# A planner's order for a hybrid decoder layer: corrected prices, and 260 listed shifts of its priorities

## The chip, the core and the metric

The kernel runs on one core of a Trainium2 chip. A core has five engines that matter here, each with its own row of instructions that it runs strictly in order: PE (TensorE, matmuls; its weight loads are shown apart as PEld), DVE (VectorE), ACT (ScalarE), POOL (GpSimd) and SP (SyncE, which here does nothing but issue DMA transfers). Engines wait for one another by semaphores. The metric is the device time of one execution in microseconds (us), the median over several runs.

## The reference, cut to what matters

One decoder layer over a prompt of 2048 tokens and 64 sample tokens (8 sequences of 8, which continue caches of 2048 keys). One input projection feeds two mixers; their gated outputs are joined by one output projection.

```python
h = rmsnorm(x, norm_w)
z = h @ w_in
q, k, v, qb, kb, vb, g_lr, gate_a, gate_b = jnp.split(z, split_points(), axis=-1)
q = rope(rmsnorm(heads(q, H_A), q_norm_w), pos)          # 8 heads x 64
k = rope(rmsnorm(heads(k, H_A), k_norm_w), pos)
o_a = attend(q, k, v)       # windows (128, 1), (512, 4), (2048, 16), joined by their softmax denominators
log_a = jax.nn.log_sigmoid(g_lr @ w_gate_up + b_gate) / GATE_TAU
o_b, s_fin = gla_chunked(qb * DK_B ** -0.5, kb, vb, log_a, s0)   # gated linear attention, 4 heads
o_b = rmsnorm(o_b, gla_norm_w)
mixed = jnp.concatenate([o_a * silu(gate_a), o_b * silu(gate_b)], axis=-1)
y = x + mixed @ w_out
```

Beside y the layer returns the new keys and values and the GLA states.

## The kernel before

**Tiles.** The prompt is cut into 16 tiles of 128 tokens, and "s" is the tile of the sample. Activations and weights are split into two fp16 parts, high and low, so each projection takes three products per 128 rows of depth: high x high, high x low, low x high (L1745). The projections come in the blocks q, k, v, qkb (queries and keys of the GLA), g (gate a and the low-rank gate), vb and gb (gate b); their sums are acc_q, acc_k and so on. Weights are loaded as f32 (wr_...), scaled, and written by ACT (L1275) and DVE (L1276) as w_....

**Attention.** Rotated q and k go to memory (qp_d, kp_d) and come back transposed by SP: kk (L1457) and qq (L1471) for branches 1 and 2, in four slabs m = 0 to 3 of 512 tokens; T_q and T_k (L1556, L1558) for the 16 residues of branch 3. A unit is s (scores, PE, L1025), mask and exponential (DVE L1033, ACT L1036), t (transposes on PE, L1043), a split into fp16 parts (ACT, DVE or POOL), O (PE, L1058), and a store to o_d.

**Dots.** The sample's scores over its cached keys are no matmuls. For each sequence and step SP loads a row of queries to all partitions (qb, L1610) and blocks of keys (k, L1612 and L1615); POOL multiplies (pr, L1600) and DVE adds up (sck, L1601). There are 128 such dots.

**GLA.** Eight pieces e0 to e7 of 256 tokens, and one of the sample. The decays are seven steps of POOL (kq_e, L839) with PE's scores between (sc_e, L872). Each 128-token chunk ends in O_0 to O_15 (PE, L1911 and L1917), a norm over ACT and DVE (gla_out, L909 to L916: osq, oss, rr, ob_c), and a store to ob_d (L917).

**Output.** For each tile, combine(t) (L2122 to L2165) loads the three branch results (oc, L2125), the GLA result (obl), and the two gates (gwl, gal), weighs them on DVE, ACT and POOL, and writes mix; parts_of splits it (mt, L2063 and L2064), PE transposes it (tm, L2073), and Y (L2108) is the output projection. The sample's attention over its cached values (R L2291, OS L2357, values sv_b) is woven in between.

**What sets the order.** All instructions are recorded first. Then the class Plan reads their dependences, gives each a price (busy: how long its engine is held; late: when its result is there; lands: for a DMA, the time from the end of its bytes to its signal), and makes a list schedule. order runs a model of the five engines and picks, whenever one is free, the ready instruction with the smallest priority. backward runs the same from the end and gives new priorities, the latest place of each instruction. settle repeats the two and returns an order for each engine; fix then ties each engine's instructions into that order. Nothing of the computation is touched. In the kernel before, settle makes eight rounds, plays each order on four copies of the program with randomly lengthened prices (other, replay), and keeps the best:

```python
    plan = Plan(tc, nc)
    plan.fix(plan.settle(8, 500.0, 1.2, 50.0, 10.0))
```

## Time and profile before

| | |
|---|---|
| runs | 1297.75, 1304.37, 1305.67 us; median 1304.37 |
| profiled execution | 1306.69 us, of which 1304.9 us span from its first to its last instruction |
| mean granted PE clock | 0.986 |
| PE busy | 1222.5 us, 94% |
| DVE, ACT, POOL busy | 961.1 us (74%), 819.1 us (63%), 551.1 us (42%) |
| HBM | 198 GB/s over the span |

The profile is of one execution. A line number is that of the kernel before; in the kernel after, the lines behind the planner's prices stand 3 further down (L1457 is L1460, L2108 is L2111). A busy PE is one with a matmul in its pipeline, which is not always PE at its peak. A wait is put down to the engine or transfer that came last. The order of the span is: projections q, k, v to about 160 us, attention with the qkb and g projections as filler to about 815, GLA with vb and gb as filler to about 1040, output projection with the sample's attention to the end.

### The profile page before, as it was taken

Reading aid. Unit: us, or ns where it says so; the run is one execution under the profiler, and the core shown is the slowest. Engines: PE = TensorE matmul, PEld = TensorE weight load, DVE = VectorE, ACT = ScalarE, POOL = GpSimd, SP = SyncE. Lnnn points to the kernel's source line nnn. Section 1 sums busy time; section 2 is a strip of 40 time slices with the busy share of each in tenths; the row PEclk is TensorE's granted clock in tenths of the full one; section 3 lists DMA queues with packets and bytes.
Section 4 is the critical chain, followed back from the end, with each engine's and each line's share of the span. In section 5 each row is a group of like instructions: output and inputs, shape, how many; then the busy total and the mean of one; then the engine's idle time right before and its main releaser. Section 6 shows DMA issues by size and latency. Waiting matters only on the chain.

```text
span 1304.9 us, 26224 instructions
## 1 busy us (share of the span) xinstructions
PE 1222.5 (94%) x8942; PEld 726.2 (56%) x8942; DVE 961.1 (74%) x2450; ACT 819.1 (63%) x2191; POOL 551.1 (42%) x475
## 2 busy tenths in 40 slices
PE   4999989999998989999999999999999959999998
PEld 2444465666576556766666656665665425445443
DVE  7897888989889648777778558787778485567641
ACT  6655598888499759968678435678788532223220
POOL 0145435555655225643434777545433142233410
PEclk9999999999999989999999999999999969999999
DMA  8579945876944977799999877554335499989822
GB/s 293 187 212 247 252 152 114 223 190 196 218 133 143 222 226 252 228 253 274 260 245 245 246 206 202 156 171 149 118 118 171 146 330 397 342 331 364 297 94 75
DMA packets 235833, 283.09 MB, mean 217 GB/s; under 512 B 116193, under 2 KB 146866, under 8 KB 232626
## 3 DMA queue, kind: packets, MB, share of 16 engines
q1 hardware_dynamic: 235698, 281.40, 72.2%
q8 instruction: 71, 1.16, 0.4%
q14 instruction: 64, 0.52, 0.1%
HBM read 183.02 MB, written 75.24 MB: 198 GB/s over the span
## 4 chain that ended last, share of the span: by engine, by line
PE 36%; DVE 9%; DMA 8%; ACT 7%; issue 4%; POOL 4%; SPq 1%; DVEq 0%; POOLq 0%; ACTq 0%
PE Y L2108 11%; PE acc_qkb L1745 5%; PE acc_gb L1745 3%; POOL pr L1600 2%; PE OS L2357 2%; PE acc_vb L1745 2%; ACT p L1036 2%; PE s L1025 2%; PE t L1043 1%; PE acc_g L1745 1%; PE O L1058 1%; DMA oc<-o_d 1%; DMA qb<-q_d 1%; DMA T_q<-qp_d 1%; PE sc_e L872 1%
## 5 line engine op out<-in xcount | busy, mean ns | idle before, releaser
L1600 POOL TENSOR_TENSOR pr<-k,qb 128x512 f32<-128x512 f32 x128 | 166.8, 1303 | 190.8 <-DVE sck L1601 107.9
L1745 PEld LDWEIGHTS <-hr 128*128 128x128 f16 x1824 | 174.2, 99 | 115.1 <-issue 12.2
L1036 ACT ACTIVATE p<-p,o 128x256 f32<-128x256 f32 (+1 forms) x384 | 172.7, 454 | 39.9 <-DVE o L1033 35.7
L1745 PEld LDWEIGHTS <-hl 128*128 128x128 f16 x1248 | 119.5, 98 | 120.9 <-issue 9.2
L2108 PE MATMUL Y<-w_o,mh 128*128 128x512 f16 x768 | 181.4, 381 | 1.9 <-ACT mh L2074 1.4
L1010 POOL TENSOR_TENSOR pt<-p,pt 128x512 f16<-128x512 f32 (+1 forms) x80 | 95.1, 1190 | 109.8 <-ACT pt L1009 91.1
L1058 PE MATMUL O<-v,pt 128*128 128x128 f16 x1200 | 131.0, 219 | 10.0 <-POOL pt L1010 3.5
L1043 PE MATMUL t<-ident,p 128*128 128x128 f32 x600 | 125.3, 283 | 2.4 <-ACT p L1036 1.0
L1601 DVE TENSOR_REDUCE sck<-pr 128x8 f32<-128x512 f32 x128 | 87.1, 680 | 54.9 <-POOL pr L1600 54.5
L2108 PEld LDWEIGHTS <-mh 128*128 128x128 f16 x768 | 71.9, 98 | 85.4 <-issue 9.8
L1745 PE MATMUL acc_g<-w_g,hr 128*128 128x256 f16 (+1 forms) x768 | 117.4, 277 | 0.5 <-DVE za L1447 0.2
L1745 PE MATMUL acc_v<-w_v,hl 128*128 128x512 f16 x384 | 115.7, 384 | 2.3 <-ACT zs_q L1320 1.5
L1058 PEld LDWEIGHTS <-pt 128*128 128x128 f16 x1200 | 92.0, 98 | 42.8 <-POOL pt L1010 8.1
L1745 PE MATMUL acc_k<-w_k,hl 128*128 128x512 f16 x384 | 110.4, 379 | 0.5 <-DVE vp L1407 0.5
L1745 PE MATMUL acc_q<-w_q,hl 128*128 128x512 f16 x384 | 107.1, 379 | 2.1 <-DVE za L1447 1.1
L1745 PE MATMUL acc_vb<-w_vb,hr 128*128 128x512 f16 x384 | 103.5, 382 | 4.8 <-DVE so_g L1294 4.8
L1033 DVE CUSTOM_DVE_ANT_0 p<-s,m3w,scl_s 128x128 f32<-128x128 f32 (+1 forms) x256 | 88.4, 394 | 15.8 <-PE s L1025 7.1
L1745 PE MATMUL acc_gb<-w_gb,hr 128*128 128x512 f16 x384 | 96.0, 383 | 0.0
L2156 POOL TENSOR_TENSOR tc<-oc,w 128x512 f32<-128x512 f32 x32 | 44.2, 1400 | 112.7 <-DVE w L2148 67.4
L1025 PE MATMUL s<-kk,qq 128*128 128x256 f16 (+1 forms) x512 | 82.8, 268 | 8.7 <-DMA kk<-kp_d 4.7
L1043 PEld LDWEIGHTS t<-ident,p 128*128 128x128 f32 x600 | 74.8, 141 | 28.4 <-ACT p L1036 12.4
L1745 PE MATMUL acc_qkb<-w_qkb,hr 128*128 128x512 f16 x288 | 79.0, 383 | 0.1
(528 smaller groups left out, 2545.7 us busy)
## 6 DMA issues: line engine op xcount, KB each, us to landing
k<-in_cache_k_win SPq DMA_DIRECT2D x104, 256.0 KB
sv_b<-in_cache_v_win SPq DMA_DIRECT2D x24, 1024.0 KB
hr<-h_d SPq DMA_DIRECT2D x44, 512.0 KB
qb<-q_d SPq DMA_DIRECT2D x64, 256.0 KB
oc<-o_d SPq DMA_DIRECT2D x48, 264.0 KB
o_d<-o SPq DMA_DIRECT2D x64, 132.0 KB
x<-in_x_prompt SPq DMA_DIRECT2D x16, 512.0 KB
h_d<-hl SPq DMA_DIRECT2D x16, 512.0 KB
```

What stands on the lines that cost most here:

```text
L1010: POOL.tensor_tensor(l, f, h, ALU.subtract)
L1025: PE.matmul(s_ps[:, i * w : (i + 1) * w], q, k, start=(n == 0), stop=(n == len(prods) - 1),)
L1033: DVE.tensor_tensor_reduce(s[:, sl], s_ps[:, sl], mask, neg, BIG, ALU.add, ALU.min, nmf(i))
L1036: ACT.activation(s[:, sl], s[:, sl], AF.Exp, bias=nmf(i), scale=-1.0, accum_out=denf(i))
L1043: PE.transpose(p_ps[:, i * P : (i + 1) * P], t["s"][:, i * P : (i + 1) * P], ident[:])
L1058: PE.matmul(o_, t["pt"][:, c, (i * nb + b) * P : (i * nb + b + 1) * P], vf(i, b), start=(n == 0), stop=(n == 2 * nb - 1),)
L1600: POOL.tensor_tensor(pr[:], kt, qt, ALU.mult)
L1601: DVE.tensor_reduce(out, pr[:].rearrange("p (u k d) -> p u k d", u=2, k=4), AX.X, ALU.add)
L1745: PE.matmul(z, a_[:, k, :], w[:, p_, k, cols], start=(k == 0 and i == 0), stop=(k == KT - 1 and i == 2),)
L2108: PE.matmul(Y[:], a_[:, k, :], w_[:, part, k, :512], start=(i == 0), stop=(i == len(prods) - 1),)
L2156: eng.tensor_tensor(t_[:], oc[:, g, :, 0:64], w[:, g].unsqueeze(2).to_broadcast([P, NH, HD]), ALU.mult,)
L2357: PE.matmul(OS[32 * x : 32 * x + 32, 0:256], ps(x), vs_[bb][:, 256 * u : 256 * u + 256], start=(i == 0), stop=(i == 13),)
```

## The change

Prices in Plan.price are corrected: the bytes of a transposing DMA and its landing are shorter; a DMA with one row spread to all partitions costs 3.16 times as much; the others depend on whether they write to memory and how long their rows are; a DVE instruction with two 16-bit inputs is 110 ns later; DVE and ACT are held 5 ns longer; and POOL's cheap case is told by the innermost dimension alone.

The perturbed copies (other, replay) and the choice among rounds go. settle now makes seven rounds with slightly other margins, and then goes through a list of 260 numbers. Each number seeds a generator that draws one instruction and one of four sets: all instructions that belong to the same tile (half of the draws), the instruction alone, the instructions of its engine within a reach of 10 to 100 us that write tiles of the same kind, or all of its engine within that reach. The priorities of the set are shifted together by a normal number times 1, 3, 10 or 30 us. After all shifts one order is made and fixed. The program is the same instruction for instruction; only the five rows are other.

```diff
--- before.py
+++ after.py
@@ -320,8 +320,8 @@
                 if kind == "InstDmaTransposeAnt":
                     total = cells(ts[0]) * ts[0].ap[0][1] * 2
                     busy = 1400.0 if total < 500000 else 2800.0
-                    late = 18.0 * total / 256 / 16
-                    self.lands[len(self.busy)] = 2200.0
+                    late = 11.2 * total / 256 / 16
+                    self.lands[len(self.busy)] = 1900.0
                 else:
                     nd = max(
                         len([x for x in list(a.ap) if x[1] != 1]) for a in (ts[0], os_[0])
@@ -331,7 +331,14 @@
                     total = cells(os_[0]) * list(os_[0].ap)[0][1]
                     total *= 2 if os_[0].dtype in (F16, BF16) else 4
                     late = total / r / 16 * (7 + r * 0.0377)
-                    self.lands[len(self.busy)] = 2300.0 if space(os_[0]) == "DRAM" else 2900.0
+                    if space(os_[0]) == "DRAM":
+                        more, lands = 0.98, 1870.0
+                    elif list(ts[0].ap)[0][0] == 0:
+                        more, lands = 3.16, 1700.0
+                    else:
+                        more, lands = (1.05, 2390.0) if r >= 4096 else (1.11, 2325.0)
+                    late *= more
+                    self.lands[len(self.busy)] = lands
                 busy += 25
                 late *= self.traffic
             else:
@@ -364,12 +371,14 @@
                     else:
                         late = (205 if by_row else 145) + (0.52 if sbuf else 1.042) * n
                         lock = sbuf
-                    busy = late - 80
+                    if len(wide) >= 2 and all(a.dtype in (F16, BF16) for a in wide):
+                        late += 110
+                    busy = late - 75
                 elif e == "Activation":
                     late = (160 if space(ts[0]) == "PSUM" else 190) + 0.836 * cells(o) if ts else 60
                     if len([a for a in ts[1:] if cells(a) == 1]) and cells(o) > 1:
                         late += 90
-                    busy = late - 105
+                    busy = late - 100
                     if len(os_) > 1:
                         busy += 92
                         late += 85
@@ -381,7 +390,10 @@
                     elif kind == "InstTensorCopy":
                         late = 130 + 1.0 * n
                     else:
-                        spread = any(s == 0 and c > 1 for a in ts for s, c in list(a.ap)[1:])
+                        spread = any(
+                            d[-1][0] == 0
+                            for d in ([x for x in list(a.ap)[1:] if x[1] > 1] for a in ts) if d
+                        )
                         half = any(a.dtype in (F16, BF16) for a in ts)
                         late = 180 + (1.68 if spread else 1.92 if half else 2.12) * n
                     busy = late - 45
@@ -622,55 +634,46 @@
                 released(x)
         return place
 
-    def other(self, seed):
+    def moved(self, seed):
 
         import random
 
-        r, q = random.Random(seed), Plan.__new__(Plan)
-        q.__dict__.update(self.__dict__)
-        q.late, q.busy, q.lands = list(self.late), list(self.busy), dict(self.lands)
-        for n in range(self.real):
-            if self.eng[n] == "SP":
-                q.late[n] *= 0.4 + 0.6 * r.expovariate(1)
-                q.lands[n] += 400 * (r.expovariate(1) - 0.5)
-            elif self.eng[n] != "PE":
-                more = r.choice((0, 0, 0, 30))
-                q.late[n] += more
-                q.busy[n] += more
-        return q
-
-    def replay(self, out):
-
-        q = Plan.__new__(Plan)
-        q.__dict__.update(self.__dict__)
-        q.then, q.behind = [list(x) for x in self.then], [set(x) for x in self.behind]
-        for order in out.values():
-            for a, b in zip(order, order[1:]):
-                if a not in q.behind[b]:
-                    q.behind[b].add(a)
-                    q.then[a].append(b)
-        return q.order([0.0] * len(self.dep), 0.0)[0]
-
-    def settle(self, rounds, land, traffic, cross, bias, others=4):
-
-        true = Plan.__new__(Plan)
-        true.__dict__.update(self.__dict__)
+        r = random.Random(seed)
+        n, kind = r.randrange(self.real), r.random()
+        by = r.gauss(0, 1) * r.choice((1e3, 3e3, 1e4, 3e4))
+        if kind < 0.5:
+            return self.mates[self.leaf[n]], by
+        if kind < 0.6:
+            return [n], by
+        reach, own = r.choice((1e4, 3e4, 1e5)), self.stem[n]
+        return [
+            x for x in range(self.real)
+            if self.eng[x] == self.eng[n] and abs(self.base[x] - self.base[n]) < reach
+            and (kind > 0.85 or self.stem[x] == own)
+        ], by
+
+    def settle(self, rounds, land, traffic, cross, bias, steps):
+
         self.rank()
-        true.nxt, true.then = self.nxt, self.then
-        others = [true.other(k) for k in range(others)]
         self.lands = {n: x + land for n, x in self.lands.items()}
         self.late = [
             x * (traffic if self.eng[n] == "SP" else 1.0) for n, x in enumerate(self.late)
         ]
         self.cross = cross
-        prio, best = [-f for f in self.rank()], None
+        prio = [-f for f in self.rank()]
         for _ in range(rounds):
-            out = self.order(prio, bias)[1]
+            self.order(prio, bias)
             prio = [-x for x in self.backward(self.start)]
-            end = sum(o.replay(out) for o in others)
-            if best is None or end < best[0]:
-                best = end, out
-        return best[1]
+        self.leaf = [next((t for t, w, m in reversed(a) if w), "?") for a in self.acc]
+        self.stem = [t.rstrip("_0123456789") for t in self.leaf]
+        self.mates, self.base = {}, list(prio)
+        for n, t in enumerate(self.leaf):
+            self.mates.setdefault(t, []).append(n)
+        for seed in steps:
+            some, by = self.moved(seed)
+            for x in some:
+                prio[x] += by
+        return self.order(prio, bias)[1]
 
     def fix(self, out):
 
@@ -2417,8 +2420,43 @@
 
         weave(out, [sample_attention(), 4 * 9])
 
+    steps = (
+        798993397, 379503271, 976436735, 990016090, 697217584, 129675417, 778155539, 369111627,
...
+        933499419, 856040043, 620662419, 525063118, 526738383,
+    )
     plan = Plan(tc, nc)
-    plan.fix(plan.settle(8, 500.0, 1.2, 50.0, 10.0))
+    plan.fix(plan.settle(7, 600.0, 1.15, 60.0, 10.0, steps))
 
 
 # ---- launch: one core; inputs and outputs as the reference has them ----
```

**Place 1: the end of the gb projection.** On PE, the last matmuls of the last GLA chunk, O_15 (O_13304), among the gb matmuls. acc_gb_13985 is gb tile 12, acc_gb_14061 gb tile 13; tiles 14 and 15 follow. Before:

```order
L1745 LDWEIGHTS hr_13839
L1745 MATMUL acc_gb_14061<-w_gb,hr_13839 128x512
L1917 MATMUL O_13304<-vb_13297,full 128x128 x2
L1745 LDWEIGHTS hr_13839
L1745 MATMUL acc_gb_14061<-w_gb,hr_13839 128x512
L1745 LDWEIGHTS hr_13839
L1745 MATMUL acc_gb_14061<-w_gb,hr_13839 128x512
```

After:

```order
L1748 LDWEIGHTS hr_13798
L1748 MATMUL acc_gb_13985<-w_gb,hr_13798 128x512
L1914 MATMUL O_13304<-Sbd_9605,kq_e_13053 128x256
L1920 MATMUL O_13304<-vb_13297,full 128x128 x2
L1914 MATMUL O_13304<-Sbd_9605,kq_e_13053 128x256
L1920 MATMUL O_13304<-vb_13297,full 128x128 x2
L1748 LDWEIGHTS hr_13798
L1748 MATMUL acc_gb_13985<-w_gb,hr_13798 128x512
```

O_15 stands one gb tile earlier. Up to the first output transpose 52 gb matmuls follow it before, 90 after.

On SP, the same place: ob_c_13329 is the result of O_15, oc_13929 with obl, gwl and gal the loads of the first combine, gw_14097 the finished gate of gb tile 13, gw_14022 of tile 12. Before:

```order
L1391 DMA gw_d<-gw_14022 128x512
L917 DMA ob_d<-ob_c_13329 128x512
L1391 DMA gw_d<-gw_14097 128x512
L2125 DMA oc_13929<-o_d 128x528 x3
L2128 DMA obl_13934<-ob_d 128x512
L2130 DMA gwl_13936<-gw_d 128x512
L2132 DMA gal_13938<-ga_d 128x512
L2125 DMA oc_14025<-o_d 128x528 x2
```

After:

```order
L1394 DMA gw_d<-gw_13918 128x512
L920 DMA ob_d<-ob_c_13329 128x512
L2276 DMA Sc_15377<-sc_d 128x2x128
L2128 DMA oc_13929<-o_d 128x528 x3
L2131 DMA obl_13934<-ob_d 128x512
L1394 DMA gw_d<-gw_14022 128x512
L2133 DMA gwl_13936<-gw_d 128x512
L2135 DMA gal_13938<-ga_d 128x512
```

The loads oc and obl stand right behind the store of O_15 and one load for the sample (Sc); the store of gate 13 is no longer ahead of them.

**Place 2: the keys of the last slab, m = 3.** On SP, T_q and T_k for branch 3, qq and kk for branches 1 and 2. Before:

```order
L1556 DMA_TRANSPOSE T_q_7921<-qp_d 128x8x128
L1558 DMA_TRANSPOSE T_k_7923<-kp_d 128x8x128
L1457 DMA_TRANSPOSE kk<-kp_d 128x8x128
L1517 DMA o_d<-o_2_1_2_6115 128x264
L1517 DMA o_d<-o_2_1_3_6204 128x264
L1502 DMA v_3_0_2_6867<-vp_d 128x512
L1373 DMA zqk_d<-zq_6592 128x512
L1182 DMA hr_6776<-h_d 128x2048
L1471 DMA_TRANSPOSE qq_1_7049<-qp_d 128x4x128
L1562 DMA v_0_7814<-vp_d 128x1024
L1457 DMA_TRANSPOSE kk<-kp_d 128x8x128
```

After:

```order
L1559 DMA_TRANSPOSE T_q_7797<-qp_d 128x8x128
L1460 DMA_TRANSPOSE kk<-kp_d 128x8x128
L1185 DMA hr_6440<-h_d 128x2048
L1376 DMA zqk_d<-zq_6249 128x512
L1505 DMA v_3_0_0_6670<-vp_d 128x512
L1561 DMA_TRANSPOSE T_k_7799<-kp_d 128x8x128
L1474 DMA_TRANSPOSE qq_1_7049<-qp_d 128x4x128
L1460 DMA_TRANSPOSE kk<-kp_d 128x8x128
L1520 DMA o_d<-o_2_1_1_5940 128x264
L1561 DMA_TRANSPOSE T_k_7923<-kp_d 128x8x128
```

Before, the last two kk stand behind both T_k's. After, the third stands ahead of both, and the last (row 385 of SP before, 375 after) between them.

**Place 3: the first decay of the GLA.** On POOL, kq_e_10021 is piece e0 in decay, pr are the dots (pr_7_4 is sequence 7, step 4), and Ac_e, prod_e and gT_e belong to the GLA too. Before:

```order
L1600 TENSOR_TENSOR pr_7_0_7903<-k_7_0_7899,qb_0_7897 128x512
L1600 TENSOR_TENSOR pr_7_0_7906<-k_7_0_7901,qb_0_7897 128x512
L839 TENSOR_TENSOR kq_e_10021<-kq_e_10021,d_e_10050 128x256
L1600 TENSOR_TENSOR pr_7_4_8007<-k_7_4_8005,qb_4_8003 128x512
L839 TENSOR_TENSOR kq_e_10021<-kq_e_10021,sums_e_10053 128x128x2
L1600 TENSOR_TENSOR pr_7_4_8010<-k_7_0_7901,qb_4_8003 128x512
L839 TENSOR_TENSOR kq_e_10021<-kq_e_10021,sums_e_10053 128x64x4
L791 MEMSET gT_e_11313 17x256
L773 TENSOR_TENSOR prod_e_10875<-zqk_e_10871 128x512
L839 TENSOR_TENSOR kq_e_10021<-kq_e_10021,sums_e_10053 128x32x8
L1600 TENSOR_TENSOR pr_7_1_8110<-k_7_1_8106,qb_1_8104 128x512
L839 TENSOR_TENSOR kq_e_10021<-kq_e_10021,sums_e_10053 128x16x16
```

After:

```order
L842 TENSOR_TENSOR kq_e_10021<-kq_e_10021,d_e_10050 128x256
L783 TENSOR_TENSOR Ac_e_10448<-ident_9596,dd_e_10446 128x512
L1603 TENSOR_TENSOR pr_6_6_7629<-k_6_6_7627,qb_6_7625 128x512
L1603 TENSOR_TENSOR pr_6_6_7632<-k_6_2_7529,qb_6_7625 128x512
L842 TENSOR_TENSOR kq_e_10021<-kq_e_10021,sums_e_10053 128x128x2
L1603 TENSOR_TENSOR pr_6_3_7721<-k_6_3_7717,qb_3_7715 128x512
L794 MEMSET gT_e_11313 17x256
L776 TENSOR_TENSOR prod_e_10875<-zqk_e_10871 128x512
L842 TENSOR_TENSOR kq_e_10021<-kq_e_10021,sums_e_10053 128x64x4
L1603 TENSOR_TENSOR pr_6_3_7724<-k_6_3_7719,qb_3_7715 128x512
L842 TENSOR_TENSOR kq_e_10021<-kq_e_10021,sums_e_10053 128x32x8
L1603 TENSOR_TENSOR pr_6_7_7807<-k_6_7_7805,qb_7_7803 128x512
```

The first decay stands nine rows earlier (296, not 305), and with it go earlier dots: the last three steps of sequence 6 and all of sequence 7, two dots each, now stand behind it: 22 dots, where 14 did.

31 rows, old and new, of the table steps are left out of this document.

## The prediction

> **What bounds the kernel now.** I read the busy line of the page first, then the table of stretches, the waits where TensorE is not busy, and the chain through the largest of these.
>
> ```profile
> PE 1222.5 (94%) x8942; PEld 726.2 (56%) x8942; DVE 961.1 (74%) x2450; ACT 819.1 (63%) x2191; POOL 551.1 (42%) x475
> ```
>
> PE is the bound, with 1222.5 of 1304.9 us: the other 82.4 us is all that better waits can give. The change leaves every matmul in place, so a gain has to come out of these, or out of the pipeline breaks inside the busy time. The columns below are stretch and length; busy time of PE, PEld, DVE, ACT, POOL; then the granted clock, the DMA share and GB/s.
>
> ```profile
> 130.50:163.10 32.60, 32.52 (x163) 15.36 (x161) 26.38 (x47) 18.35 (x43) 14.38 (x9) 1.00 0.95 252
> 163.10:195.70 32.60, 28.45 (x247) 19.63 (x245) 27.08 (x101) 31.28 (x114) 12.65 (x12) 1.00 0.50 152
> 195.70:228.40 32.70, 30.92 (x232) 18.70 (x230) 26.34 (x69) 26.57 (x84) 16.53 (x13) 1.00 0.53 114
> 456.70:489.30 32.60, 27.90 (x180) 17.77 (x179) 14.79 (x47) 18.64 (x55) 8.03 (x7) 0.90 0.80 226
> 815.60:1011.30 195.70, 187.95 (x1601) 117.44 (x1599) 154.02 (x391) 152.87 (x380) 84.45 (x92) 0.98 0.47 147
> 1043.90:1076.50 32.60, 16.57 (x109) 8.86 (x110) 29.34 (x60) 11.26 (x18) 15.04 (x10) 0.69 0.92 330
> 1059.00:1240.00 181.00, 178.94 (x1351) 87.14 (x1350) 118.30 (x258) 48.42 (x75) 59.71 (x44) 0.99 0.93 349
> ```
>
> The hole is at 1043.9: 16.0 us idle in one stretch, with the clock at 0.69. Next come 4.7 us at 456.7, 4.15 and 1.8 us at 163.1 and 195.7, where ACT is full (31.28 of 32.60), and 7.75 us spread over the GLA. Behind 1059 PE is full. The waits that name the two sharp holes, over 1040 to 1062 and over 465 to 472 (total, times, longest):
>
> ```profile
> PE tm L2073 <- ACT mt L2063: 17.7, 1, 17.7
> ```
>
> ```profile
> PE s L1025 <- DMA kk<-kp_d: 4.7, 1, 4.7
> ```
>
> **A. From the gb projection to the output projection.** The chain through the hole, with start, length and what ran, and SP's issues in it:
>
> ```profile
> 1029.06 9.50 PE acc_gb L1745 x44
> ...
> 1038.61 5.02 DMA oc<-o_d
> ...
> 1056.72 0.69 DVE mix L2163
> ...
> 1057.44 1.06 ACT mt L2063
> ```
>
> ```profile
> 1034.37 0.33 SPq L917 DMA_DIRECT2D ob_d<-ob_c  x1
> 1035.31 0.32 SPq L1391 DMA_DIRECT2D gw_d<-gw  x1
> 1035.68 1.39 SPq L2125 DMA_DIRECT2D oc<-o_d  x3
> ```
>
> The last GLA chunk, O_15, ends on PE at 1029.06. Its norm and store take until 1034.37, a gw store whose POOL product is late holds SP, and the loads of the first combine start at 1035.68. The first output transposes (tm) run 17.7 us after PE's last work, at 1058.8, that is 29.8 us after O_15. Nothing but gb matmuls covers this: in the old order 52 stand behind O_15, at 9.50/44 = 0.216 us each 11.2 us. The new order has 90, so 19.4 us: +8.2. In the new order SP's loads follow ob_d with one short load between, not that gw store: of the 1.31 us from ob_d to oc I take 0.6 off. And the two ACT steps of O_15's norm (rr) no longer stand behind steps of a gate each:
>
> ```profile
> 1036.45 0.72 ACT L1298 ACTIVATE sa_gb<-sa_gb,ones 128x512 f32<-128x512 f32 x1
> ```
>
> Two of these, up to 0.72 us each, make 1.2. The hole becomes 17.7 - 8.2 - 1.8 = 7.7, **A = -10**.
>
> This has a floor of its own. On DVE the last gate (so_gb15) now stands ahead of mix of tile 0, and on ACT its last step stands ahead of mt:
>
> ```profile
> 1040.29 0.75 DVE L1294 TENSOR_SCALAR so_gb<-acc_gb,wi_gb 128x512 f32<-128x512 f32 x1 [1.30 <-PE acc_gb L1745]
> ...
> 1043.15 0.69 DVE L1302 CUSTOM_DVE_ANT_0 so_gb<-so_gb,sa_gb 128x512 f32<-128x512 f32 x1
> ```
>
> From the last gb result to the end of that gate are 1043.84 - 1040.29 = 3.55 us; mix (0.69) and mt (1.06) make 5.3 us that no order of PE hides. So A lies between -12.4 and 0 (0 if the oc loads land as late after the last gb as before).
>
> The cold clock stays: 0.69 in the stretch, and a hole of 5 to 8 us I price like one of 17.7, at no change. The Trainium skill (TensorE: Matmul & The Clock Gate, "What's actually happening") says that an idle window of about 3.4 us is enough to halve the clock, and about as much work to release it; the 0.69 agrees. By that page a hole of 7.7 us saves nothing of the cold stretch, as I have it.
>
> **B. Attention, third slab of keys (m = 3).** SP's issues there, and then, from the chain, the landing of the fourth kk:
>
> ```profile
> 440.50 1.30 SPq L1457 DMA_TRANSPOSE kk<-kp_d  x1
> ...
> 447.00 3.59 SPq L1558 DMA_TRANSPOSE T_k<-kp_d  x1
> 450.64 1.31 SPq L1457 DMA_TRANSPOSE kk<-kp_d  x1
> ...
> 456.76 3.12 SPq L1558 DMA_TRANSPOSE T_k<-kp_d  x1
> 459.92 1.31 SPq L1457 DMA_TRANSPOSE kk<-kp_d  x1
> ```
>
> ```profile
> 465.79 5.30 DMA kk<-kp_d
> 471.13 1.87 PE s L1025 x8
> ```
>
> The four kk are issued at 440.5, 450.6, 459.9 and 465.8; the last lands 5.30 us later, and s starts at 471.13. The new order puts three of them ahead of both T_k's (3.59 and 3.12 us) and the fourth between them, ten rows of SP earlier than it was, since the last kp half leaves DVE earlier. But s too stands some 16 us of PE's rows earlier, with qkb matmuls moved behind it. The 4.7 us can go entirely, or come back whole as the same landing against an earlier reader. I take two thirds: **B = -3** (0 to -4.7).
>
> **C. First attention units (m = 0).** Before 163.1 ACT is busy 18.35 of 32.60, after it 31.28. The new order begins the units some 11 us of PE's rows earlier and puts the last q and k tiles and the sample's projections (matmuls without such waits) between them. The two holes sum to 5.9 us. A third of them goes: **C = -2**; at best -5, at worst +2, since the fourth kk of m = 0 is issued just before its reader and a landing of 5.30 us behind 2 to 3 us of other work costs that.
>
> **D. GLA and the dots.** POOL's dots over 815 to 915 (count, busy time, mean ns, idle before them):
>
> ```profile
> L1600 POOL TENSOR_TENSOR pr<-k,qb 128x512 f32<-128x512 f32 x11 | 14.5, 1317 | 12.0 <-DVE sck L1601 7.1 <-DMA k<-in_cache_k_win 2.7 <-DMA ga_d<-so_g 2.2
> ```
>
> Behind the first GLA decay (kq_e) 22 dots stand now instead of 14. Eight more at 1.32 us are 10.5 us in POOL's row, of which POOL is busy 84.45 of 195.70 there. They fit, and the first decay comes nine rows earlier. GLA matmuls also stand in somewhat longer runs. Of the 7.75 us idle I take a fifth: **D = -1.5** (-8 to +10.5).
>
> **E. Output stage.** Sample attention (OS) interrupts the output matmuls:
>
> ```profile
> 1107.84 0.55 PE OS L2357 x2
> ...
> 1108.93 1.86 PE OS L2357 x30
> ```
>
> Between the runs of 2 and of 30 lie 28 matmuls in 1.31 us, 0.047 us each, so a run costs about 0.46 us beside its work. OS has 26 runs on PE before and 15 after, R 7 and 12. Eleven fewer and five more are six runs, 2.8 us; shorter tm runs give no sure price. **E = -3** (-5 if only the OS runs count, +2 if only R's).
>
> The start (identity loaded first, transposes reordered) and the tail (last Y and stores, the same) I take at 0, +-1.
>
> **Sum.** -10 - 3 - 2 - 1.5 - 3 = -19.5. The profiled execution took 1306.69 (span 1304.9 and 1.8 around it): 1306.7 - 19.5 = **1287**. It lies 2.3 above the median of the runs shown, 1304.37, and a run of 1297.75 lies below both, so the median may come out at 1285; I stay with 1287. Within 1% of 1304.37 is 1291.3 to 1317.4, about what a measurement of this kernel can tell from no change.
>
> **Rivals.**
>
> *Absorbed.* The new PE order spends each gain on an earlier reader: s waits for the same landing, only sooner, the first units wait for the fourth kk, the oc loads start earlier but land in a fuller queue (DMA share 0.92). Then A is half, -5; B, D, E 0; C +2: 1306.7 - 3 = 1304, and with A kept whole 1299; I take 1301. For it: the holes at 163 and 466 are waits for data, which a shift of the order does not shorten. Against: SP's rows do move with them. Chance 0.25.
>
> *The output stage is bound by DMA.* From 1059 to 1240 it moved 349 GB/s at a share of 0.93. If only 0.07 is free, the 181 us cannot shrink below 168, which A and E do not ask; but if the sample values (sv_b) already set the pace, E is 0 and a part of A, its 6 us of earlier start, is waited for later: 1306.7 - 4 - 6.5 = 1296. Chance 0.06. The Trainium skill (DMA: Bandwidth & Descriptors, "Where 436 GB/s comes from") states about 358 GB/s per core as the limit between memory and SBUF; by it 349 leaves 3%, and 181 us could not go below 176. The trace speaks against that:
>
> ```profile
> 1076.50:1109.20 32.70, 32.45 (x333) 16.44 (x335) 18.07 (x53) 8.38 (x18) 8.39 (x7) 1.00 1.01 397
> ```
>
> That stretch moved 397 GB/s, with PE busy 32.45 of 32.70 us.
>
> *Slower: dots in front of the decays.* POOL runs in order. Over the whole execution its dots waited 36.3 us in 9 waits for their keys:
>
> ```profile
> POOL pr L1600 <- DMA k<-in_cache_k_win: 36.3, 9, 20.8
> ```
>
> If each of the eight later dots meets such a wait (4.0 us) besides its 1.3 us, the decays behind it, and the whole GLA chain to O_15, come up to 8 x 5.3 = 42 us later, at least 10.5. PE then waits within the GLA, since the gb matmuls stand behind O_15. The forecast plus 10.5 is 1298, plus 42 is 1329; it is slower from 30 us on, that is, if most of the eight wait. Three quarters of the full price gives 1319. For it: the dots' loads share SP with the GLA's. Against: only 2.7 us of such waits in 815 to 915. Chance 0.08.
>
> *More.* A at its floor (-12.4), B -4.7, C -5, D -5, E -5: 1306.7 - 32 = 1275. Chance 0.07.
>
> **How the numbers follow.** My forecast, 1279 to 1291.3, has 0.54. With "more" that is 0.61 faster; absorbed and DMA make 0.31 within 1%; 0.08 slower. The range runs from 1271, a little under "more", to 1305, the upper end of "absorbed": that leaves out the slower case and the edges. The forecast's own range is 1279 to 1296.
>
> **What would show it.** A: PE's wait for mt of tile 0 at 6 to 9 us, not 17.7, and the last gb matmuls some 19 us long behind O_15. B: the wait of s for kk at 465 gone or under 2 us. C: PE busy over 130 to 228 up by 2 us or more. D: POOL's wait for keys within the GLA still a few us, PE idle there under 8. E: fewer OS runs, the stage from first tm to the end 3 us shorter. I am wrong if the hole before tm stays above 13 us, if s waits for kk in new places by more than 3 us, or if the GLA's end lies later than before.

## The result, and the profile after

The changed kernel takes 1263.6 us (median of 4 runs, 1262.71 to 1264.7) against 1304.43 us before: a ratio of 0.970, with a 95% interval of 0.966 to 0.973. That is 41 us or 3.0% faster, where 17 us were forecast, and below the range (1271 to 1305). The two profiled executions, on which everything below rests, lie 44 us apart (spans 1304.9 and 1260.9). The kernel before, timed again beside the experiments, gave medians of 1300.6 to 1304.3 us, so a difference of 3 us between two kernels below means little; e2, e3 and e6 had one run each of 2 to 3.4 ms, which the ratios leave out.

The busy line of the page after:

```profile
PE 1202.4 (95%) x8942; PEld 723.7 (57%) x8942; DVE 956.1 (76%) x2450; ACT 817.8 (65%) x2191; POOL 549.0 (44%) x475
```

The instructions and their busy times are the same to within 1% on DVE, ACT and POOL. PE's busy time fell by 20 us, and the time in which PE is not busy by 24 (82.4 to 58.5). So only about half of the gain lies in time that the page shows as idle. The stretches of after that answer to those shown of before, with the same columns (those at 446, 791.2 and 1016.9 begin within 2 us of the same work as in before; the one at 1007.6 begins just ahead of the hole, where that of before began 3 us inside it):

```profile
130.50:163.10 32.60, 31.04 (x196) 17.53 (x195) 28.89 (x67) 24.12 (x65) 14.03 (x10) 1.00 1.00 265
163.10:195.70 32.60, 28.50 (x262) 20.34 (x262) 27.06 (x100) 31.69 (x113) 13.53 (x13) 1.00 0.33 103
195.70:228.40 32.70, 32.67 (x197) 17.03 (x195) 24.62 (x56) 22.11 (x66) 15.14 (x12) 1.00 0.67 165
446.00:478.60 32.60, 32.56 (x254) 21.85 (x252) 23.60 (x75) 27.23 (x81) 17.32 (x14) 1.00 0.96 270
791.20:980.00 188.80, 185.66 (x1622) 117.80 (x1619) 159.82 (x388) 153.11 (x383) 91.30 (x98) 1.00 0.51 164
1007.60:1040.20 32.60, 22.18 (x134) 10.75 (x132) 31.36 (x62) 10.91 (x15) 20.27 (x14) 0.79 0.83 298
1016.90:1196.00 179.10, 176.41 (x1390) 88.33 (x1391) 111.84 (x245) 48.38 (x75) 53.27 (x40) 0.98 0.91 341
```

PE is idle for 10.4 us in the stretch at 1007.6, of which the hole is 8.8, and hardly at all in that of the fourth kk. The stretch at 163 has as much idle time as before. The waits of PE after, first over the whole span, then over 130 to 520:

```profile
PE tm L2076 <- ACT mt L2066: 8.8, 1, 8.8
```

```profile
PE s L1028 <- DMA kk<-kp_d: 1.8, 2, 1.5
```

Of these 1.8 us only 0.3, in one wait, lies behind 395 us, in the third slab (m = 3); the rest is in the first units.

**A view that shows the rest.** PE's busy time fell although its matmuls are the same, so it holds more than their own work: breaks between them, and slower ones. So I take from the two traces only the starts of the 8942 matmuls. Each form of matmul weighs as much as the lower quartile of its start-to-start times in before. These weights sum to 1089.6 us in both kernels. Whatever the order, the time at which a kernel has done a given sum can then be compared with the other's. The table gives the difference to before, in us, of the time spent between fixed sums; the heads are the times at which before passes them. Negative is gained.

| kernel (profiled execution) | 0-175 | 175-397 | 397-515 | 515-732 | 732-990 | 990-1071 | 1071-end | sum |
|---|---|---|---|---|---|---|---|---|
| changed | -0.3 | -11.5 | -8.4 | -4.2 | -9.4 | -6.9 | -3.5 | -44.3 |
| e1: new prices, no shifts | 0.0 | -11.7 | -4.3 | +0.9 | -4.1 | -2.1 | +0.6 | -20.7 |
| e6: e1 with six rounds | +6.8 | -15.1 | -6.9 | +7.1 | -5.3 | -1.3 | +4.8 | -9.9 |
| e2: before with new prices | +8.3 | -12.5 | -6.1 | +4.6 | -6.4 | +0.7 | -0.4 | -11.8 |
| e5: old prices, new rounds, no shifts | +3.0 | -3.7 | -0.7 | +5.3 | -6.1 | -0.6 | -2.2 | -5.0 |
| e10: e5, transposes new | +2.5 | -3.4 | -3.9 | +11.1 | -4.8 | 0.0 | +0.4 | +1.9 |
| e11: e5, copies new | -2.9 | -1.7 | -0.2 | +19.1 | -8.1 | +0.9 | -2.6 | +4.7 |
| e12: e5, engines new | +2.3 | -8.7 | -1.8 | +5.3 | -5.2 | +1.0 | -2.4 | -9.5 |
| e15: e5, POOL new | +2.3 | -10.7 | +1.6 | +8.8 | -5.8 | -2.0 | +2.0 | -3.9 |
| e16: e5, DVE and ACT new | +4.2 | -9.1 | +0.6 | +1.1 | +8.3 | -2.2 | -2.5 | +0.5 |
| e3: old prices, all shifts | +0.8 | -1.1 | -1.1 | +6.5 | -0.3 | -1.6 | +0.9 | +4.1 |
| e4: new prices, other shifts | +5.0 | -4.7 | -2.4 | +7.3 | +2.7 | +1.7 | +12.3 | +21.8 |
| e7: first 130 shifts | +0.6 | -9.6 | -6.6 | -4.2 | -8.0 | -6.6 | +1.0 | -33.5 |
| e8: the 102 late shifts | +0.1 | -12.1 | -7.1 | +3.8 | -8.3 | -7.4 | +1.0 | -29.9 |
| e9: the 158 early shifts | -0.2 | -10.8 | -7.5 | +5.1 | -7.0 | -0.5 | -1.8 | -22.7 |
| e13: e1, last GLA piece earlier | +1.7 | -10.1 | -4.7 | +1.0 | -5.7 | -1.9 | +5.4 | -14.3 |
| e14: e1, last GLA piece later | 0.0 | -10.9 | -2.4 | -1.7 | -7.5 | +5.7 | +7.9 | -8.8 |
| e17: changed, mix first | -2.6 | -11.2 | -7.5 | -5.9 | -9.7 | -4.4 | -3.2 | -44.4 |

The stages are: projections; attention m = 0 to 2; attention m = 3; branch 3 and the first of the GLA; GLA; the hole; the output stage. One execution against another is good to a few us in a cell, as runs of one kernel differ by some us.

### The profile page after: what moved, and what is told of

It reads as the page before. It is cut to its first block, busy times and chain, and to the rows that moved or that the text cites. A ratio compares the mean times of both kernels' runs of the same rounds, so it can differ in the third digit from the quotient of the medians.

```text
span 1260.9 us, 26211 instructions
## 1 busy us (share of the span) xinstructions
PE 1202.4 (95%) x8942; PEld 723.7 (57%) x8942; DVE 956.1 (76%) x2450; ACT 817.8 (65%) x2191; POOL 549.0 (44%) x475
## 4 chain that ended last, share of the span: by engine, by line
PE 53%; ACT 15%; DVE 15%; DMA 8%; issue 6%; SPq 2%; POOL 2%; DVEq 0%; ACTq 0%; POOLq 0%
PE Y L2111 13%; PE acc_v L1748 5%; PE acc_qkb L1748 4%; PE acc_k L1748 4%; PE acc_q L1748 3%; PE acc_vb L1748 3%; PE t L1046 3%; ACT p L1039 3%; PE O L1061 3%; PE s L1028 3%; PE acc_g L1748 3%; DMA o_d<-o 2%; PE OS L2360 2%; DMA qb<-q_d 2%; DVE p L1036 2%
## 5 line engine op out<-in xcount | busy, mean ns | idle before, releaser
L2111 PE MATMUL Y<-w_o,mh 128*128 128x512 f16 x768 | 178.5, 383 | 2.4 <-ACT mh L2077 1.3
L1013 POOL TENSOR_TENSOR pt<-p,pt 128x512 f16<-128x512 f32 (+1 forms) x80 | 91.4, 1142 | 147.2 <-ACT pt L1012 124.1
L1061 PE MATMUL O<-v,pt 128*128 128x128 f16 x1200 | 135.6, 219 | 5.4 <-DVE pt L1009 1.9
L1748 PE MATMUL acc_g<-w_g,hr 128*128 128x256 f16 (+1 forms) x768 | 112.0, 276 | 0.0
L1748 PE MATMUL acc_v<-w_v,hl 128*128 128x512 f16 x384 | 108.5, 383 | 0.4 <-ACT zs_q L1323 0.4
L1748 PE MATMUL acc_k<-w_k,hl 128*128 128x512 f16 x384 | 104.4, 379 | 0.5 <-DVE vp L1410 0.4
L1748 PE MATMUL acc_vb<-w_vb,hr 128*128 128x512 f16 x384 | 100.9, 379 | 3.9 <-DVE so_g L1297 3.4
L1748 PE MATMUL acc_q<-w_q,hl 128*128 128x512 f16 x384 | 102.4, 379 | 0.1
L1036 DVE CUSTOM_DVE_ANT_0 p<-s,m3w,scl_s 128x128 f32<-128x128 f32 (+1 forms) x256 | 87.7, 394 | 12.1 <-PE s L1028 4.7
L1028 PE MATMUL s<-kk,qq 128*128 128x256 f16 (+1 forms) x512 | 87.7, 264 | 4.8 <-DVE o L1036 2.9
L1046 PEld LDWEIGHTS t<-ident,p 128*128 128x128 f32 x600 | 74.6, 141 | 26.8 <-ACT p L1039 11.5
```

What stands on the lines that cost most here:

```text
L1013: POOL.tensor_tensor(l, f, h, ALU.subtract)
L1028: PE.matmul(s_ps[:, i * w : (i + 1) * w], q, k, start=(n == 0), stop=(n == len(prods) - 1),)
L1036: DVE.tensor_tensor_reduce(s[:, sl], s_ps[:, sl], mask, neg, BIG, ALU.add, ALU.min, nmf(i))
L1046: PE.transpose(p_ps[:, i * P : (i + 1) * P], t["s"][:, i * P : (i + 1) * P], ident[:])
L1061: PE.matmul(o_, t["pt"][:, c, (i * nb + b) * P : (i * nb + b + 1) * P], vf(i, b), start=(n == 0), stop=(n == 2 * nb - 1),)
L1748: PE.matmul(z, a_[:, k, :], w[:, p_, k, cols], start=(k == 0 and i == 0), stop=(k == KT - 1 and i == 2),)
```

## The experiments

### What carries it: prices, rounds or shifts

Two theories: S, the listed shifts carry the gain; P, the corrected prices do. e1 takes the shifts away:

```diff
-    plan.fix(plan.settle(7, 600.0, 1.15, 60.0, 10.0, steps))
+    plan.fix(plan.settle(7, 600.0, 1.15, 60.0, 10.0, ()))
```

> The changed kernel with an empty list: corrected prices, seven rounds, no shifts. Theory S (the shifts carry the gain): 1290 to 1305, within 1% of before, and the hole before the first output transposes near 18 us. Theory P (the truer prices carry it): 1263 to 1278, with the hole already near 9 us.

Measured 1286.79 us, ratio 0.989 (0.986 to 0.992). Neither theory: by the times about a third of the gain is there without shifts, by the table nearly half, and the hole is hardly shorter than the 17.7 us of before:

```profile
PE tm L2076 <- ACT mt L2066: 16.4, 1, 16.4
```

e2 is the kernel before with the corrected prices, all hunks of the change in the method price, and nothing else of it:

```diff
-                    late = 18.0 * total / 256 / 16
-                    self.lands[len(self.busy)] = 2200.0
+                    late = 11.2 * total / 256 / 16
+                    self.lands[len(self.busy)] = 1900.0
...
-                    busy = late - 105
+                    busy = late - 100
...
```

> The kernel before with the corrected prices alone; its eight rounds and the choice among them on four perturbed copies stay. Theory S: 1290 to 1305. Theory P: 1263 to 1278. If this lies more than 8 us below the same prices with seven rounds and no choice, the choice that the change drops was worth something.

Measured 1297.55 us, ratio 0.997 (0.995 to 0.999): by its time S, but the table shows the same 12 us gained in 175-397 as in e1, and 8 lost ahead of it. It lies 11 us above e1, so nothing shows that the choice among rounds, which the change drops, was worth something.

e3 is the changed kernel with the same hunks taken back, so that the 260 shifts act on other priorities:

```diff
-                    late = 11.2 * total / 256 / 16
-                    self.lands[len(self.busy)] = 1900.0
+                    late = 18.0 * total / 256 / 16
+                    self.lands[len(self.busy)] = 2200.0
...
```

> The changed kernel with the old prices: the same 260 numbers, drawn on priorities made from other prices. Theory S in its strict form (the shifts were selected for one set of priorities): no gain left, 1295 to 1320. Theory S in a loose form (shifts that are good in themselves): 1270 to 1285. Theory P: at or above before, 1300 to 1320.

Measured 1310.87 us, ratio 1.008 (1.005 to 1.011): the strict form of S. As a whole the list is worth nothing on other priorities. One part of it acts there too, since the longest wait of tm is as short as in the changed kernel:

```profile
PE tm L2064 <- ACT mt L2054: 10.2, 2, 9.1
```

But the stretch of the hole, 990-1071, wins only 1.6 us in e3: other stops take its place.

e4 takes 260 other shifts:

```diff
-            some, by = self.moved(seed)
+            some, by = self.moved(seed + 1)
```

> The changed kernel with every listed number raised by one: 260 shifts of the same kinds and sizes, not the listed ones. Theory S: worse than no shifts, 1300 to 1340, since unselected shifts break a good order. Theory P: like no shifts within 10 us.

Measured 1333.05 us, ratio 1.025 (1.021 to 1.029), 46 us above no shifts, as S had it. So which numbers stand in the list is worth 70 us between e4 and the changed kernel.

### How far a plan moves by itself

e5 is e1 with those hunks taken back as in e3, and e6 is e1 with one round less:

```diff
-    plan.fix(plan.settle(7, 600.0, 1.15, 60.0, 10.0, ()))
+    plan.fix(plan.settle(6, 600.0, 1.15, 60.0, 10.0, ()))
```

> The changed kernel with the old prices and no shifts: seven rounds and the new margins alone. Corrected prices alone gave 1297.6 and prices with the new rounds 1286.8, against 1300.6 before. If prices and rounds are two separate causes that add up, this gives 1300.6 - (1297.6 - 1286.8) = 1290. If the prices make the attention's 12 us and the rest is which of many orders the planner happens to end on, it gives 1295 to 1312, with no gain between 175 and 400 us of the span.

Measured 1300.3 us, ratio 0.998 (0.996 to 1.000): 3.7 us gained in 175-397 where e1 has 11.7, and no separate effect of rounds and margins that adds up.

> Corrected prices, no shifts, six rounds and not seven: a change that carries no knowledge of the chip. It measures how far the planner's result moves by itself. If rounds and margins matter as such, within 3 us of 1286.8. If the result is a draw among orders, 5 to 15 us away, with the gain between 175 and 400 us of the span still there.

Measured 1299.28 us, ratio 0.998 (0.996 to 1.000), 12.5 us above seven rounds: a draw among orders. Yet the gain in 175-397 is there (-15.1). So the total of a plan says little about a price; a stage that nearly all plans with it win says more.

### Which price makes the attention's 12 us

Three kernels take e5 and put in one part of the new prices each. e10 has the transposing DMAs:

```diff
-                    late = 18.0 * total / 256 / 16
-                    self.lands[len(self.busy)] = 2200.0
+                    late = 11.2 * total / 256 / 16
+                    self.lands[len(self.busy)] = 1900.0
```

e11 has the other DMAs:

```diff
-                    self.lands[len(self.busy)] = 2300.0 if space(os_[0]) == "DRAM" else 2900.0
+                    if space(os_[0]) == "DRAM":
+                        more, lands = 0.98, 1870.0
...
+                    self.lands[len(self.busy)] = lands
```

e12 has the lines on DVE, ACT and POOL, which are those of e15 and e16 below.

> Old prices, seven rounds, no shifts, and of the corrections only that of the transposing DMAs. Every plan made with the corrected prices so far gained 12 to 15 us of PE's progress between 175 and 400 us of the span and 4 to 9 us more up to 515, the two with the old prices 0 to 4 and 0 to 1. If the price of the transposes makes this (the keys and queries come through them): 12 us or more gained in 175 to 400, time 1283 to 1293. If another correction does: less than 4 us there, 1295 to 1306.

> Old prices, seven rounds, no shifts, and of the corrections only that of the other DMAs (stores land earlier, loads earlier, broadcast rows cost three times as much). If this makes the attention's gain: 12 us or more in 175 to 400 us of the span, 1283 to 1293. If not: less than 4 us there, 1295 to 1306.

> Old prices, seven rounds, no shifts, and of the corrections only those of DVE, ACT and POOL (110 ns more for two 16-bit inputs, 5 ns more of holding, POOL's cheap case narrowed, so that its splits of the probabilities cost more). If this makes the attention's gain, since POOL and DVE do those splits: 12 us or more in 175 to 400 us, 1283 to 1293. If not: less than 4 us there, 1295 to 1306.

One run each: 1308.57, 1311.94 and 1297.63 us, the first two above both ranges that were given. In 175-397 they won 3.4, 1.7 and 8.7 us; the old prices alone won 3.7. So it is not the DMA prices by themselves. The 8.7 of e12 lies between its two cases, 12 or more and less than 4. Then the engines' part in two. e15 has POOL's new test alone:

```diff
-                        spread = any(s == 0 and c > 1 for a in ts for s, c in list(a.ap)[1:])
+                        spread = any(
+                            d[-1][0] == 0
+                            for d in ([x for x in list(a.ap)[1:] if x[1] > 1] for a in ts) if d
+                        )
```

e16 has the lines on DVE and ACT alone:

```diff
-                    busy = late - 80
+                    if len(wide) >= 2 and all(a.dtype in (F16, BF16) for a in wide):
+                        late += 110
+                    busy = late - 75
...
-                    busy = late - 105
+                    busy = late - 100
```

> Old prices, seven rounds, no shifts, and of the corrections only POOL's: its rope steps (t_qk and ct_qk) and gates cost some 20% more, since the cheap case is told by the innermost dimension. The engines' corrections together won 8.7 us of PE's progress between 175 and 400 us of the span, the old prices with the same rounds 3.7. If it is POOL's price: 8 us or more there, and 1650 matmuls or more in 175 to 400 us, where the old prices have 1624. If it is DVE's or ACT's, or only the planner's luck: 0 to 5 us, 1610 to 1635 matmuls. Time 1290 to 1305.

> Old prices, seven rounds, no shifts, and of the corrections only those of DVE and ACT (5 ns more of holding each, 110 ns for two 16-bit inputs). If POOL's price makes the attention's gain: 0 to 5 us between 175 and 400 us, 1610 to 1635 matmuls there. If these do: 8 us or more, 1650 or more. Time 1290 to 1310.

One run each: 1302.79 and 1307.59 us. The stretch 175 to 400 of the span, first of before, then of e5, e15, e16 and the changed kernel:

```profile
175.00:400.00 225.00, 213.59 (x1601) 137.58 (x1599) 197.53 (x508) 186.49 (x556) 121.10 (x92) 1.00 0.67 175
```

```profile
175.00:400.00 225.00, 216.03 (x1624) 139.13 (x1622) 193.87 (x514) 188.59 (x563) 120.01 (x91) 0.99 0.67 176
```

```profile
175.00:400.00 225.00, 219.12 (x1675) 142.89 (x1673) 193.84 (x528) 193.98 (x579) 118.71 (x92) 1.00 0.68 175
```

```profile
175.00:400.00 225.00, 218.14 (x1655) 142.00 (x1653) 194.87 (x523) 191.46 (x572) 122.77 (x93) 0.99 0.64 177
```

```profile
175.00:400.00 225.00, 219.67 (x1656) 143.17 (x1654) 198.46 (x517) 191.13 (x560) 125.72 (x97) 1.00 0.68 183
```

PE issues 1655 to 1675 matmuls in 225 us instead of 1601 to 1624, with ACT 3 to 5 us busier than in e5. Each half alone does what was expected of the one that carries the gain, so neither is the one: either does it, and the two do not add (10.7 and 9.1 alone, 8.7 together). Of the plans that have no new engine price, five with before, none won more than 3.7 us here; thirteen of the fourteen with one won 8.7 to 15.1, the one with the other shifts (e4) 4.7. So the gain in this stage goes with the engines' prices. The split is less clean where the stage ahead is counted in: from 0 to 397 the plans without a new engine price win 0 to 4.6 us, those with one 4.2 to 13.8, and e4 loses 0.3. Which line of the prices carries it, and through which wait, stays open. POOL's price, at least, is nearer to the trace of before than the old one. Its rope steps there:

```profile
L1344 POOL TENSOR_TENSOR t_qk<-zs_q,ct_qk 128x1024 f32<-128x1024 f32 x12 | 28.8, 2402 | 28.4 <-ACT zs_q L1320 14.3 <-DVE qs_q L1321 10.8 <-DVE ra_x L758 2.6
```

They take 2402 ns; by the formula in price the old test gave 180 + 1.68 x 1024 = 1900, the new one gives 180 + 2.12 x 1024 = 2351.

### Whether the shifts act each for itself

```diff
+        cut = min(x for x, t in zip(self.base, self.stem) if t == "kq_e")
         for seed in steps:
             some, by = self.moved(seed)
+            if not self.base[random.Random(seed).randrange(self.real)] >= cut:
+                continue
```

e8 has this, e9 the same with < for >=. e7 has steps[:130].

> Only the 102 of the 260 shifts whose drawn instruction has a priority from the first GLA decay on; the other 158 are left out. If the shifts act where they are drawn: the hole before the first output transposes is 8 to 11 us, not 16.4, and the time is 1286.8 less the 16 to 19 us that the full list wins behind 815 us of the span, 1268 to 1272. If the list works only as a whole, each shift having been kept on the order that the ones ahead of it had made: 1280 to 1300.

> Only the 158 shifts whose drawn instruction has a priority ahead of the first GLA decay. If the shifts act where they are drawn: the hole before the output stays near 16 us and the time is 1286.8 less 4 to 9 us, 1278 to 1283, and the gains of the two parts add up to the 23 us of the whole list. If the list works only as a whole: 1285 to 1305.

Measured 1279.48 us (0.983; 0.981 to 0.986) and 1280.01 us (0.984; 0.981 to 0.987). Each wins 7 us over e1 and together 14 of the 23, so the parts do not add up. The time of e9 alone is what acting in place would give; that of e8 lies between its two cases, on the side of the whole. In the hole they do what was drawn there: 8.9 us with the late shifts, 16.4 with the early ones:

```profile
PE tm L2081 <- ACT mt L2071: 8.9, 1, 8.9
```

```profile
PE tm L2081 <- ACT mt L2071: 16.4, 1, 16.4
```

But 515-732, where the full list gains 4.2, comes out at +3.8 and +5.1. No plan without shifts is as good as before there (+0.9 to +19.1); the full list and its first half are better, and so, by 1.7, is e14 below, whose one shift lies elsewhere.

> The changed kernel with the first 130 of the 260 numbers. In its order 90 gb matmuls stand behind O_15, as with all. The whole list wins 23 us over no shifts; the 102 late ones alone won 7, the 158 early ones alone 7. If the list is a chain, each step kept on the order made by the ones ahead of it, its first half is a whole by itself and wins more than the late or the early ones do: 12 to 20 us, 1267 to 1275, with a hole of 9 us. If the parts only interfere: 1275 to 1285.

Measured 1275.0 us, ratio 0.978 (0.976 to 0.980): 12 us over e1, on the line between the two expectations, and better than either part of the list that was cut by place. With e3 and e4 this fits a chain, in which a step counts on the order that the ones ahead of it made; that each was kept for such a reason is argued, not shown.

### The hole before the output stage

e13 has no list, but one shift:

```diff
-        for seed in steps:
-            some, by = self.moved(seed)
-            for x in some:
-                prio[x] += by
+        for x, t in enumerate(self.leaf):
+            if "e7" in t or "c14" in t or "c15" in t or t[:5] in ("O_14_", "O_15_", "U_15_"):
+                prio[x] -= 10e3
```

> Corrected prices, seven rounds, and instead of the 260 shifts one: everything of the last GLA piece and of the norms of its two chunks gets a priority 10 us earlier. In the order 71 gb matmuls then stand behind O_15, where 51 did without shifts and 90 with all. If the hole before the output stage is the chain behind O_15 less the gb matmuls that cover it: 16.4 - 20 x 0.216 = 12.1 us, and the time 1286.8 - 4.3 = 1282.5 as far as the rest of the order stays. If the hole is set by the loads (oc) or by DVE's own row: 16 us as before.

e14 has += for -=.

> Corrected prices, no shifts but one: the last GLA piece with the norms of its two chunks gets a priority 10 us later. Six gb matmuls then stand behind O_15, where 51 did (hole 16.4 us) and 71 with the opposite shift (hole 11.2). If each matmul behind O_15 covers its 0.216 us: a hole of 16.4 + 45 x 0.216 = 26 us. If loads or DVE set the hole: 16 to 18 us. Time 1287 + 10 = 1297 if nothing else moves.

Measured 1290.55 us (ratio 0.990; 0.987 to 0.993) and, in one run, 1298.38 us. The holes, of e13 and of e14:

```profile
PE tm L2075 <- ACT mt L2065: 11.2, 1, 11.2
```

```profile
PE tm L2075 <- ACT mt L2065: 22.7, 1, 22.7
```

With the number of gb matmuls that the traces have between O_15 and the first tm (51 for before, where the count ahead of the result was 52):

| kernel | matmuls behind O_15 | hole, us |
|---|---|---|
| e14 | 6 | 22.7 |
| e2 | 48 | 18.6 |
| e11 | 50 | 17.8 |
| before, e4 | 51 | 17.7 |
| e1, e6, e9 | 51 | 16.4 |
| e5, e10, e12, e15, e16 | 57 or 58 | 16.5 to 17.4 |
| e13 | 71 | 11.2 |
| changed, e8, e7 | 90 | 8.8, 8.9, 9.1 |
| e3 | 92 | 9.1 |

From 51 to 71 the hole shrinks by 5.2 us (4.3 expected), from before to the changed kernel by 8.9 over 39 matmuls, 0.228 us each against the 0.216 that one takes. Downwards it grows less, by 6.3 and not 9.7 over 45, which is between the two cases of that expectation; why is open. That the hole follows the number of matmuls behind O_15 is shown; from 48 to 58 other things move it by 1 to 2 us. A shorter hole is not yet a faster kernel: e13 is 4 us slower than e1 and not 4 faster, since it is 4.8 us worse from 1071 on, in a stage whose priorities the shift does not change, and e3 with 92 is slower than before.

e17 edits the finished rows of the changed kernel:

```diff
+        for e, first, last in (("DVE", "mix_0_", ("so_gb15", "w_1_", "mix_1_", "dw_1_")),
+                               ("Activation", "mt_0_", ("sa_gb15", "w_1_"))):
...
+            out[e] = [n for i, n in enumerate(row[: k + 1]) if i not in some] + keep + row[k + 1 :]
```

> The changed kernel, and in its finished rows one edit at the hole before the output stage: on DVE the last gate's second step and the second tile's w, mix and dw go behind mix of tile 0, on ACT the last gate and the second tile's w behind mt of tile 0. If the last gate ahead of mix sets the hole that is left (8.8 us), as the forecast's floor has it: mix can start when POOL's sum is there, 1013.4 and not 1015.1, the hole is 7.2 us, and the time 1262. If the loads or the sum on POOL set it: 8.8 us and 1263.6. If the second tile pays for it: a hole of 7.2 and a time at or above 1263.6.

Measured 1266.09 us, ratio 0.972 (0.970 to 0.975): no gain. Its waits:

```profile
PE tm L2089 <- ACT mt L2079: 7.7, 1, 7.7
PE tm L2089 <- DVE mt L2080: 3.0, 1, 3.0
```

The first wait is 1.1 us shorter and a second of 3.0 appears: the low half of the same tile (mt on DVE) stands behind what was moved and starts at 1017.25, hardly before the 1017.38 of the changed kernel. The last case of the expectation, only that the first tile's own second half pays and not the second tile. The times of the two orders are not told apart (the interval of the changed kernel is 0.966 to 0.973); in the stretch of the hole e17 wins 4.4 us and the changed kernel 6.9.

## Why the prediction was right or wrong

In the terms of the table the profiled execution gained 44.3 us and the sum had 19.5. C is short by 9.5, D by 7.9, B by 5.4, a stage without a term by 4.2; A came out 3 smaller. The step that failed in C, D and B is the same: each was bounded by idle time that the page shows, in a few stretches or one wait. The forecast named breaks inside the busy time as a second source and gave them no term.

**The start and the tail, 0.** Right for the start: -0.3 up to 175. The tail is not told apart from E.

**A, -10 with the hole at 7.7.** Right in mechanism, and the hole is 8.8 us, 8.9 shorter; the stretch around it won 6.9. That the size fits is in part two errors that offset each other. The 1.8 us that I took off the chain for SP and the norm did not come. PE and SP of the changed kernel:

```profile
986.68 1.03 PE L1748 MATMUL acc_gb<-w_gb,hr 128*128 128x512 f16 x4
...
1016.92 1.03 PE L2076 MATMUL tm<-ident,mt 128*128 128x128 f16 x8 [8.84 <-ACT mt L2066]
```

```profile
992.62 1.45 SPq L2128 DMA_DIRECT2D oc<-o_d  x3
```

The first gb matmul behind O_15 starts at 986.68, tm at 1016.92: 30.2 us, where before had 29.7 (1028.90 to 1058.56). In return PE stays busy behind O_15 for 21.4 us and not 12.0, which is 9.4 more and not 8.2. The loads do start sooner, 5.9 us behind that matmul and not 6.8, but the end of the chain is longer. Its DVE row there:

```profile
1012.21 1.24 DVE L2147 TENSOR_TENSOR dw<-w,oc 128x24 f32<-128x24 f32 x1
1013.38 1.78 DVE L1305 CUSTOM_DVE_ANT_0 so_gb<-so_gb,sa_gb 128x512 f32<-128x512 f32 x1
1015.10 0.08 DVE L1305 DVE_READ_ACCUMULATOR2_ANT gmax_b<- 128x1 f32 x1
1015.10 0.68 DVE L2166 TENSOR_TENSOR mix<-tc,gal 128x512 f32<-128x512 f32 x1
```

The last gate does stand ahead of mix as the floor said, and takes 1.78 us where I had 0.69.

**B, -3.** Right about the wait, too small for the stage. The wait for the fourth kk went from 4.7 to 0.3 us, near the whole of it. The stage won 8.4. The step that failed is the price: one wait stood for a stage, without the slow matmuls behind the wait (see the clock below), and the 2 to 8 us that all plans with the full new prices win there had no term.

**C, -2.** Wrong, and this is the largest miss. I looked at the two stretches with idle time and left out the five behind them. In those two little changed: PE busy over 130 to 228 rose from 91.89 to 92.21 us where 2 or more was forecast, and the stretch at 163 still has PE idle for 4.1 us beside 31.69 us of ACT. The gain of 11.5 us lies in the whole of 175 to 397: by the starts, the stops above 0.4 us there went from 15 with 12.2 us to 7 with 5.5, and most of the rest is breaks of 0.15 to 0.4 us, 5.8 before and 2.4 after. The row 175 to 400 of before shows 11.4 us idle, and I did not ask for it.

**D, -1.5.** Wrong in size: -9.4. The term was a fifth of the 7.75 us idle. By the starts, PE lost 58 us against its weights in this stage before and 49 after, most of it in breaks below 0.15 us that count as busy, so idle time was no bound. Of the 9.4 us won, 3.9 lie in stops above 0.4 us, 2.2 between 0.15 and 0.4 and 3.5 below. Nor was the direction due to this change: fourteen of the seventeen other plans win 4 to 10 us here, e5 with old prices too. The order of before was poor in this stage.

**No term: 515 to 732.** Branch 3 and the first of the GLA won 4.2 us. The plans without shifts lose 1 to 19 us there: the order of before was a good one in this stage, and the list keeps and betters it.

**E, -3.** Right in number, -3.5, but its mechanism is not borne out. The trace has 15 OS runs where it had 26, and from the first tm to the end it takes 244.0 us and not 246.4. Yet the other plans have 17 to 25 OS runs (e17, with 15, apart), and their number does not sort this stage: e14 with 17 loses 7.9 us, e13 with 18 loses 5.4, e11 with 21 wins 2.6. So the fit of E is luck as far as the runs show.

**No term: the clock behind a wait.** The forecast took the cold clock of the hole as unchanged and gave B and D no price for it, though their rows showed 0.90 and 0.98. The stretches of before, up to its last matmul, in which the granted clock was half, two of them with the 3.4 us ahead:

```profile
469.90:476.70 6.80, 5.57 (x23) 3.73 (x23) 3.47 (x14) 2.33 (x9) 1.26 (x1) 0.50 1.04 366
824.90:828.30 3.40, 1.06 (x18) 0.66 (x18) 2.64 (x6) 2.74 (x7) 3.05 (x4) 1.00 1.00 339
828.30:831.70 3.40, 3.40 (x14) 2.16 (x13) 2.72 (x7) 1.05 (x3) 1.35 (x2) 0.50 0.73 163
886.30:889.70 3.40, 1.48 (x12) 0.76 (x11) 3.37 (x11) 3.35 (x12) 0.43 (x1) 1.00 0.00 0
889.70:893.20 3.50, 3.50 (x24) 1.78 (x23) 3.42 (x8) 3.48 (x12) 1.89 (x2) 0.51 0.33 47
1043.30:1063.80 20.50, 4.13 (x23) 2.56 (x24) 20.50 (x44) 7.67 (x13) 10.98 (x7) 0.50 0.87 282
```

Up to the last matmul the changed kernel has one:

```profile
1011.30:1025.00 13.70, 6.96 (x28) 3.21 (x29) 13.67 (x28) 5.05 (x8) 9.85 (x6) 0.50 0.67 223
```

By the weights of the table, the matmuls of the first stretch (behind the wait for kk) lost 2.7 us in it, those of the two GLA stretches 1.6 and 2.2. That is a part of the 8.4 of B's stage and of the 9.4 of D's, and it counts as busy. At the hole the clock went the other way: more matmuls ran at half of it, and they lost 4.6 us where before lost 3.3, though the hole is shorter. So "no change" was 1.3 us off there. This is read from one execution of each kernel, and no run changes the clock alone; the mean clock of every run agrees (0.983 to 0.990 for before, 0.991 to 0.995 for the changed kernel).

**The rivals.** "Absorbed" did not occur, nor is there a sign that DMA bound: the stage from the first tm on moved 341 GB/s, not 349, and became shorter. "Dots in front of the decays" was the wrong fear. Over 660 to 880, POOL's dots waited for keys

```profile
POOL pr L1603 <- DMA k<-in_cache_k_win: 7.1, 4, 4.3
```

7.1 us in four waits (4.6 in three over 690 to 915 of before), and the GLA gained. "More" had the right direction with 0.07, but its floors were taken from idle time, and so was the lower end of the range.

**What the forecast had right by accident.** 1287 us is what e1 measures, the kernel without the shifts. It is no evidence for the sum: e1 has none of A.

## What to carry to other kernels

Price a reordering by stages, and bound each stage by what its matmuls need from start to start, not by the idle time of a page: half of this gain lay inside "busy", some of it at half the clock behind a wait. A change of a planner's price or rounds moves the whole plan by some 10 us either way, so one timing of it proves nothing; compare the stage that the price is about, over several plans. And shifts that are listed for one set of priorities belong to it: with other prices they cost 10 us, and one other list cost 46.
